# Weight-block sums of two later products: from VectorE to accumulating DMAs between DRAM buffers

## The chip, the cores and the metric

The kernel runs on one core of one Trainium2 chip. The metric is the device time of one execution in microseconds (us); lower is better. A difference of 0.3% is 4.7 us here.

## The reference

The kernel computes one hybrid encoder block on a sequence of 1024 frames with 16 learned tokens in front, model width 1024, all in float32. Cut to what matters here:

```
h  = concat(meta, x)                                  # 1040 x 1024
proj = rmsnorm(h) @ w_in                              # q, k, v, gates of 8 heads
for heads 0..3: mLSTM memory, in chunks               # causal conv on q and k, gated state
for heads 4..7: retention, in chunks                  # rotary q and k, decaying state
mixed = concat(normalised, gated outputs of 8 heads)  # 1024 x 2048
h  = h + mixed @ w_out                                # "w" product, w_out 2048 x 1024
u  = rmsnorm(h)
a  = silu(causal_dwconv(u @ w_up)) * (u @ w_gate)     # width 2816
h  = h + a @ w_down                                   # "d" product, w_down 2816 x 1024
out = rmsnorm(h)[16:]
```

## The kernel before

Every matrix product is made in three TensorE passes on operands that are split into a rounded high part and a low remainder (ScalarE copies the high part, VectorE subtracts it to get the low part). Tile schedules the program: each engine has one queue, worked in order, and waits on semaphores. All of the kernel's DMAs but one go out on SyncE's queue (SP); GpSimd's queue (POOL) has a few memsets at the start and two multiplications at the very end.

**The mixers** take the span from the start to about 700 us. Head after head, `o_group` (output gates) and `v_group` and `qk_group` of the next head are TensorE's main work, and the chunks of the scan (`scan_a`, `scan_b`, `post_steps`) are laid between them by `merge`. `need` and `issue` load a weight tile some units ahead; the raw tiles of all these weights share two buffers (tag `raw`), so that a load waits until the tile two loads back has been used up: `raw_v` of a head waits for the `raw_m` tile that `last_two` (L179) reads on VectorE. `tables` (L527, L528) loads the decay tables A1 and A2 of heads 0 to 3 from DRAM, 512 KB each with every row sent to all partitions, and VectorE adds the mask (L532).

**The two later products** are made by `class Seven`: a block product of 2 x 2 blocks with seven products in place of eight (Strassen and Winograd's form). The product "w" (w_out) follows the mixers from about 700 us, the product "d" (w_down) ends the kernel from about 1320 us. Four of the seven products need sums of weight blocks. In block form the weights of one step k are four tiles of 128 x 512: w11, w21, w12, w22. The steps named "65" and "73" each read a pair of sums from DRAM (`sums`, [128, 1024] for each product, step name and k); "w" has 8 of k, "d" has 11, and the steps "1", "2" and "4" (`QUARTER`) read blocks as they are. `rsplit` splits the activation side, `give` (L689) adds a finished PSUM bank to the residual.

**The sums** are made during the mixers: `wsum(g, k)` is called 19 times, up to three times with each head (after q pieces 0 and 2 and k piece 1 of heads 1 to 7). It loads two rows of blocks, 512 KB each (L189, L190), makes four VectorE operations on 128 x 512 (L192 to L195; the first is ordered behind the latest rescaling of q or k, `last["qk"]`), and stores four results of 256 KB each (L197).

Of the kernel before, what the change touches and what calls it, by code (L numbers as in the profile page):

```python
# [10 lines left out]
F32 = mybir.dt.float32  # L11
F32R = mybir.dt.float32r
AF = mybir.ActivationFunctionType
ALU = mybir.AluOpType
# [3 lines left out]
P = 128  # L18
# [12 lines left out]
HB = 4 * P  # L31
# [30 lines left out]
def body(ctx, tc, h_in, vecs, cst, mask_in, rot, w_v0, w_v, w_fm, w_out, w_up, w_gate, w_down, out):  # L62
    nc = tc.nc
# [9 lines left out]
    def after(later, first):  # L73

        tc.add_manual_dep(later.ins, first.ins.name, mybir.DependencyInfo(mybir.DependencyClass.NoSync, mybir.DependencyReason.DATA),
                          reason="order")

    last = {}
    V, G = nc.vector, nc.gpsimd
# [7 lines left out]
    accp = accseg.enter_context(tc.tile_pool(name="accp", bufs=1, side="right"))  # L87
# [96 lines left out]
    sums = {(g, st, k): dram.tile([P, 2 * HB], F32, name=f"ws{g}{st}_{k}") for g, n in (("w", 8), ("d", KD)) for st in ("65", "73") for k in range(n)}  # L184

    def wsum(g, k):
        src, n = (w_out, 8) if g == "w" else (w_down, KD)
        a, b = (accp.tile([P, 2 * HB], F32, tag=f"rr{i}", name=f"ws{g}{k}_{i}") for i in range(2))
        nc.sync.dma_start(a, src[k])  # L189
        nc.sync.dma_start(b, src[k + n])  # L190
        w11, w21, w12, w22 = a[:, :HB], a[:, HB:], b[:, :HB], b[:, HB:]
        after(nc.vector.tensor_tensor(w22, w21, w22, ALU.add), last["qk"])  # L192
        nc.vector.tensor_tensor(w21, w21, w11, ALU.subtract)
        nc.vector.tensor_tensor(w11, w22, w11, ALU.subtract)
        nc.vector.tensor_tensor(w12, w12, w11, ALU.subtract)  # L195
        for st, i, x in (("65", 0, w11), ("65", 1, w22), ("73", 0, w12), ("73", 1, w21)):
            nc.sync.dma_start(sums[g, st, k][:, i * HB:(i + 1) * HB], x)  # L197

    wsums = [(g, k) for g, n in (("w", 8), ("d", KD)) for k in range(n)]

# [34 lines left out]
    def fsplit(nm, srcs):  # L235
        return wsplit(*split_tiles(nm), srcs)

    def wsplit(hi, lo, srcs):
        o = 0
        for x in srcs:  # L240
            n = x.shape[1]
            nc.scalar.copy(hi[:, o:o + n], x)  # L242
            nc.vector.tensor_tensor(lo[:, o:o + n], x, hi[:, o:o + n].bitcast(F32), ALU.subtract)  # L243
            o += n
        return hi, lo
# [29 lines left out]
    def gained(kb, t0, t1, gcol, dve=False):  # L275
        g = vec[:, gcol + kb:gcol + kb + 1]
        if dve:
            nc.vector.tensor_scalar(uh[kb][:, t0:t1], resid[:, kb, t0:t1], g, None, ALU.mult)
        else:
            nc.scalar.activation(uh[kb][:, t0:t1], resid[:, kb, t0:t1], AF.Copy, scale=g)  # L280
        return nc.vector.scalar_tensor_tensor(ul[kb][:, t0:t1], resid[:, kb, t0:t1], g, uh[kb][:, t0:t1].bitcast(F32), ALU.mult, ALU.subtract)
# [33 lines left out]
    st = mix.enter_context(tc.tile_pool(name="st", bufs=1))  # L315
# [17 lines left out]
    A1 = st.tile([P, T], F32, name="A1")  # L333
    A2 = st.tile([P, T], F32, name="A2")
# [220 lines left out]
            m.append(nc.tensor.matmul(pt, al, xh_, start=False, stop=last and k == n - 1, skip_group_check=True))  # L555
        return m[0], m[-1]

    def rsplit(x, tiles, late=False):
        hi, lo = (t[:, :x.shape[1]] for t in tiles)
        m = nc.scalar.copy(hi, x), V.tensor_tensor(lo, x, hi.bitcast(F32), ALU.subtract)  # L560
        if late:
            behind(m)
        else:
            last["rsplit"] = m
        return hi, lo

    def behind(m):

        for x, y in zip(m, last["rsplit"]):
            after(x, y)  # L570

    def half_of(u, o):
        return tuple(y[:, o * HB:(o + 1) * HB] for y in u)

    class Seven:
# [54 lines left out]
        def prep(self, t):  # L630

            if t >= len(self.steps) or t in self.ops:
                return
            st, k = self.steps[t]
            nm = f"{self.nm}{st}_{k}"
            d = self.draws.get(t, {})
            act = self.act
            if st == "4" and self.order[-1] != "4":
                if t not in self.four:
                    self.pre4(t)  # L640
                r = rsplit(act["A1", k], self.rt(st, k, 0))
                self.ops[t] = [(self.four[t], r, "x")]
            elif st == self.order[-1]:
                if k % 2 == 0:
                    self.w = d.get("w")
                w = self.four.get(t) or wsplit(*self.wlast(k), [self.w[:, k % 2 * HB:(k % 2 + 1) * HB]])
                self.ops[t] = [(w, self.rhalf(k, 0), "xy"[st == "2"])]
            elif st in self.QUARTER:
                if k % 2 == 0:
                    self.w = fsplit(nm, [d["w"]])  # L650
                r = rsplit(act[{"1": "A1", "2": "A2", "4": "A1"}[st], k], self.rt(st, k, 0))
                self.ops[t] = [(half_of(self.w, k % 2), r, "xy"[st == "2"])]
            elif st == "65":
                a1, a2, b2 = (act[q, k] for q in ("A1", "A2", "B2"))
                r5 = rsplit(a1, self.rt(st, k, 1))
                V.tensor_tensor(a1, b2, a1, ALU.subtract)
                w = fsplit(nm, [d["l"]])
                r6 = rsplit(a1, self.rt(st, k, 0))
                V.tensor_tensor(a1, a2, a1, ALU.subtract)
                self.ops[t] = [(half_of(w, 0), r6, "x"), (half_of(w, 1), r5, "y")]  # L660
            else:
                w = fsplit(nm, [d["l"]])
                r7 = rsplit(act["B1", k], self.rt(st, k, 0))
                r3 = rsplit(act["B2", k], self.rt(st, k, 1))
                self.ops[t] = [(half_of(w, 1), r7, "x"), (half_of(w, 0), r3, "y")]
            self.read(t)

# [21 lines left out]
        def give(self, st):  # L689

            for b, j0, half in self.GIVE[st]:
                for j in range(4):
                    V.tensor_tensor(self.rs(j + j0, half), self.banks[b, j], self.rs(j + j0, half), ALU.add)

        def last_quarter(self, i, done):

# [271 lines left out]
    for i, (t0, t1) in enumerate(NP):  # L968
        for kb in range(KB):
            x = gained(kb, t0, t1, V_MIX, dve=kb < 4 if i == 0 else i > 1 and kb % 4 == 0)  # L970
# [19 lines left out]
    for h in range(8):  # L990
        A = lambda c, h=h: (lambda: scan_a(h, c))
        B = lambda c, h=h: ab(h, c)
        merge([lambda b=b, p=p: o_group(h, b, p) for b in range(2) for p in range(3)],
              [A(0)] + [B(c) for c in range(4 if h < 7 else NCH)])
        if h == 7:
            break
        side = post_steps(h, 0) + [B(4), B(5), B(6)] + post_steps(h, 1) + [B(7), B(8)] + post_steps(h, 2)
        merge([lambda c=c: v_group(h + 1, c)() for c in range(NCH)], side)
        tables(h + 1)
        for kind in "qk":  # L1000
            for p in range(3):
                qk_group(h + 1, kind, p)
                if (kind, p) in (("q", 0), ("q", 2), ("k", 1)) and wsums:
                    wsum(*wsums.pop(0))
# [141 lines left out]
    for t, (st, k) in enumerate(mixw.steps):  # L1146
# [4 lines left out]
        if st == "65" and k == 1:  # L1151
            x = fp.tile([P, 4 * XW], F32, name="wm", tag="xh2", bufs=1)
# [175 lines left out]
    def up_part(i):  # L1328
        chunks = UC
        def done(m, half, c):  # L1330
            if isinstance(c, list):
                t = ftile(f"c{i}_{m}{half}")
                for x, (j0, j1) in zip(c, chunks):
                    nc.scalar.copy(t[:, j0:j1], x)
                c = t
            conv(i, m, half, c)
        return seven("up", i, chunks, done)

    def gate_part(i):
        def done(m, half, c):  # L1340
            gate(i, m, half, c[0] if isinstance(c, list) else c[:, :HALF])
        return seven("ga", i, [(2, XW)], done)
# [50 lines left out]
    for i in range(1, NPAIR):  # L1393
        u, g = up_part(i), gate_part(i)
# [8 lines left out]
        if 2 < i:  # L1403
            kb = i - 3
# [90 lines left out]
    for p in (1, 2):  # L1495
# [5 lines left out]
        else:  # L1501
            for mb in (1, 4):
                x = resid[:, mb, OP[2][0]:OP[2][1]]
# [84 lines left out]
```

## Time and profile before

| | us |
|---|---|
| median of 3 runs | 1552.7 (1549.5 to 1554.35) |
| span of the profiled execution | 1551.5 |
| PE busy (TensorE matmul) | 1518.8 |
| DVE busy (VectorE) | 1124.2 |
| ACT busy (ScalarE) | 737.2 |
| POOL busy (GpSimd) | 2.4 |
| DMA queue of SP, share of 16 engines' span | 38.2% |

The profiled execution is given by its span, from the first to the last instruction; the runs' median lies 1.2 us above it. In the views, PE is TensorE's matmuls and PEld its weight loads, a trailing q means the sequencer of an engine, L12 is a line of the kernel, "x" counts instructions, and an arrow "<-" between two names of tiles is "out from in". In a row of waits the numbers are the idle us in total, how often, and the longest.

### The profile page before, as it was taken

The numbers are of one execution on the slowest core, as the hardware profiler recorded it, in microseconds if no ns is written. First come the engines' busy times: TensorE is split into PE (matmuls) and PEld (weight loads), VectorE is DVE, ScalarE is ACT, GpSimd is POOL, SyncE is SP. The second block draws the span as 40 slices with busy tenths as digits, with TensorE's granted clock in tenths as the row PEclk, the third lists the DMA queues.
The fourth block names the chain that finished last, engine by engine and source line by source line (L and its number), as shares of the span: only waits on it lengthen the run. The fifth ranks groups of instructions, "written<-read, shape, count | busy, mean of one in ns | idle before, by whom it ended". The sixth has DMA issues, their size and how long they took to land.

```text
span 1551.5 us, 25426 instructions
## 1 busy us (share of the span) xinstructions
PE 1518.8 (98%) x9763; PEld 1395.5 (90%) x9763; DVE 1124.2 (72%) x2388; ACT 737.2 (48%) x1493; POOL 2.4 (0%) x12
## 2 busy tenths in 40 slices
PE   8999999999999999999999999999999999999997
PEld 8989999999989999998788998999999999888887
DVE  8757768696767767678867778666666666778657
ACT  7574655455243343436454455444444444434443
POOL 0000000000000000000000000000000000000000
PEclk9999999999999999999999999999999999999999
DMA  6125435263533525226542326332222224923313
GB/s 219 36 70 163 152 110 188 79 218 97 181 122 126 167 85 189 94 91 245 177 139 100 101 78 195 96 102 89 82 80 78 82 82 137 385 96 116 95 42 109
DMA packets 92441, 197.41 MB, mean 127 GB/s; under 512 B 9048, under 2 KB 31264, under 8 KB 92320
## 3 DMA queue, kind: packets, MB, share of 16 engines
q1 hardware_dynamic: 92176, 195.73, 38.2%
q8 instruction: 76, 1.25, 0.3%
q14 instruction: 45, 0.37, 0.1%
q10 hardware_dynamic: 144, 0.07, 0.0%
HBM read 146.44 MB, written 49.32 MB: 126 GB/s over the span
## 4 chain that ended last, share of the span: by engine, by line
PE 87%; DMA 5%; DVE 4%; ACT 2%; issue 1%; SPq 0%; DVEq 0%; ACTq 0%
PE pv L373 4%; PE pv L374 4%; PE pv L375 3%; PE po L385 3%; PE po L384 3%; PE po L383 3%; PE pdx L553 3%; PE pdx L555 3%; PE pdx L554 3%; PE pup_x L554 2%; PE pup_x L555 2%; PE pga_x L553 2%; PE pga_x L555 2%; PE pga_x L554 2%; PE pup_x L553 2%; DMA A<-scr 2%
## 5 line engine op out<-in xcount | busy, mean ns | idle before, releaser
L373 PE MATMUL pv<-hi_v,uh 128*128 128x256 f32 (+1 forms) x512 | 147.1, 288 | 6.1 <-DVE vl L349 1.9
L374 PE MATMUL pv<-lo_v,uh 128*128 128x256 f32 (+1 forms) x512 | 146.6, 287 | 0.0
L375 PE MATMUL pv<-hi_v,ul 128*128 128x256 f32 (+1 forms) x512 | 146.0, 286 | 0.0
L383 PE MATMUL po<-uh,hi_o 128*128 128x386 f32 (+2 forms) x384 | 125.7, 327 | 0.0
L384 PE MATMUL po<-ul,hi_o 128*128 128x386 f32 (+2 forms) x384 | 123.9, 323 | 0.0
L385 PE MATMUL po<-uh,lo_o 128*128 128x386 f32 (+2 forms) x384 | 123.6, 322 | 0.0
L373 PEld LDWEIGHTS pv<-hi_v,uh 128*128 128x128 f32 x512 | 97.8, 191 | 10.1 <-issue 2.9
L374 PEld LDWEIGHTS pv<-lo_v,uh 128*128 128x128 f32 x512 | 97.7, 191 | 0.6 <-DVE lo_v L150 0.5
L375 PEld LDWEIGHTS pv<-hi_v,ul 128*128 128x128 f32 x512 | 97.7, 191 | 0.1
L242 ACT CAST hi_up<-raw_up 128x512 fp32r<-128x512 f32 (+1 forms) x52 | 36.5, 719 | 108.2 <-PE pga_z L554 61.0
L383 PEld LDWEIGHTS po<-uh,hi_o 128*128 128x128 f32 x384 | 72.9, 190 | 0.2
L384 PEld LDWEIGHTS po<-ul,hi_o 128*128 128x128 f32 x384 | 72.8, 190 | 0.2
L385 PEld LDWEIGHTS po<-uh,lo_o 128*128 128x128 f32 x384 | 72.7, 189 | 0.1
L243 DVE TENSOR_TENSOR lo_ga<-fraw_ga,hi_ga 128x512 fp32r<-128x512 f32 (+1 forms) x52 | 41.8, 807 | 36.9 <-ACT hi_ga L242 36.8
L553 PE MATMUL pup_x<-uh_g,hi_up 128*128 128x256 f32 (+1 forms) x240 | 67.2, 282 | 1.2 <-ACT uh_g L1021 1.2
L554 PE MATMUL pup_x<-ul_g,hi_up 128*128 128x256 f32 (+1 forms) x240 | 67.4, 283 | 0.1
L243 DVE TENSOR_TENSOR lo_up<-raw_up,hi_up 128x512 fp32r<-128x512 f32 (+1 forms) x52 | 41.2, 809 | 35.1 <-ACT hi_up L242 34.3
L383 PE MATMUL pq<-uh,hi_q 128*128 128x400 f32 (+2 forms) x192 | 63.2, 329 | 3.1 <-DVE vl L349 1.9
L555 PE MATMUL pup_x<-uh_g,lo_up 128*128 128x256 f32 (+1 forms) x240 | 66.2, 282 | 0.0
L383 PE MATMUL pk<-uh,hi_k 128*128 128x400 f32 (+2 forms) x192 | 62.3, 324 | 0.5 <-DVE rq L404 0.5
L243 DVE TENSOR_TENSOR lo_d<-rd,hi_d 128x1024 fp32r<-128x1024 f32 (+1 forms) x34 | 37.7, 1112 | 34.0 <-ACT hi_d L242 34.0
L384 PE MATMUL pq<-ul,hi_q 128*128 128x400 f32 (+2 forms) x192 | 62.1, 324 | 0.0
(747 smaller groups left out, 4981.4 us busy)
## 6 DMA issues: line engine op xcount, KB each, us to landing
wsd<-w_down_d SPq DMA_DIRECT2D x22, 512.0 KB, 4.1
wsd<-wsd SPq DMA_DIRECT2D x44, 256.0 KB, 2.5
raw_up<-w_up_d SPq DMA_DIRECT2D x22, 512.0 KB, 3.7
fraw_ga<-w_gate_d SPq DMA_DIRECT2D x22, 512.0 KB, 3.6
acts<-cv SPq DMA_DIRECT2D x44, 256.0 KB, 2.0
rd<-wsd SPq DMA_DIRECT2D x22, 512.0 KB, 3.3
wsw<-w_out_d SPq DMA_DIRECT2D x16, 512.0 KB, 4.3
raw_o<-w_fm_d SPq DMA_DIRECT2D x16, 512.0 KB, 3.5
```

What stands on the lines that cost most here:

```text
L242: nc.scalar.copy(hi[:, o:o + n], x)
L243: nc.vector.tensor_tensor(lo[:, o:o + n], x, hi[:, o:o + n].bitcast(F32), ALU.subtract)
L373: nc.tensor.matmul(pv[:L, :nv], a, hi[:, o:o + nv], start=kb == 0, stop=False)
L374: nc.tensor.matmul(pv[:L, :nv], a, lo[:, o:o + nv], start=False, stop=False)
L375: nc.tensor.matmul(pv[:L, :nv], b, hi[:, o:o + nv], start=False, stop=kb == KB - 1)
L383: nc.tensor.matmul(pt[:, :n], a, uh[kb][:, t0:t1], start=kb == 0, stop=False)
L384: nc.tensor.matmul(pt[:, :n], a, ul[kb][:, t0:t1], start=False, stop=False)
L385: nc.tensor.matmul(pt[:, :n], b, uh[kb][:, t0:t1], start=False, stop=kb == KB - 1)
L553: m.append(nc.tensor.matmul(pt, ah, xh_, start=first and k == 0, stop=False, skip_group_check=True))
L554: nc.tensor.matmul(pt, ah, xl_, start=False, stop=False, skip_group_check=True)
L555: m.append(nc.tensor.matmul(pt, al, xh_, start=False, stop=last and k == n - 1, skip_group_check=True))
```

## The change

`wsum` no longer brings the blocks into SBUF. It writes the sums in DRAM by DMA alone, in a form of the seven products in which all sums are additions. For each k there are seven DMAs from DRAM to DRAM:

- on SP, two plain ones of 512 KB, which put w21 into both halves of the "65" and of the "73" pair (the source is read twice, 2 KB rows);
- on POOL, five that add to what is in DRAM: w22 to both halves of "65", w11 to both halves of "73" (512 KB each), then w11 to the first half of "65", and w22 and w12 to the first half of "73" (256 KB each).

Each accumulating DMA waits for the one before it on the same bytes. The signs that the subtractions had go to the activation side: `rsplit` gets a form with `minus` (ScalarE multiplies by -1, VectorE uses a scalar_tensor_tensor) for step "1" and for the second operand of "73", and `give` subtracts two of the banks.

```diff
     def wsum(g, k):
         src, n = (w_out, 8) if g == "w" else (w_down, KD)
-        a, b = (accp.tile([P, 2 * HB], F32, tag=f"rr{i}", name=f"ws{g}{k}_{i}") for i in range(2))
-        nc.sync.dma_start(a, src[k])
-        nc.sync.dma_start(b, src[k + n])
-        w11, w21, w12, w22 = a[:, :HB], a[:, HB:], b[:, :HB], b[:, HB:]
-        after(nc.vector.tensor_tensor(w22, w21, w22, ALU.add), last["qk"])
-        nc.vector.tensor_tensor(w21, w21, w11, ALU.subtract)
-        nc.vector.tensor_tensor(w11, w22, w11, ALU.subtract)
-        nc.vector.tensor_tensor(w12, w12, w11, ALU.subtract)
-        for st, i, x in (("65", 0, w11), ("65", 1, w22), ("73", 0, w12), ("73", 1, w21)):
-            nc.sync.dma_start(sums[g, st, k][:, i * HB:(i + 1) * HB], x)
+        w11, w21, w12, w22 = (src[k + n * kb, :, mb * HB:(mb + 1) * HB].rearrange("p (i j) -> p i j", i=1) for kb in range(2) for mb in range(2))
+        x65, x73 = (sums[g, st, k].rearrange("p (i j) -> p i j", j=HB) for st in ("65", "73"))
+        both = lambda v: v.to_broadcast([P, 2, HB])
+        for x in (x65, x73):
+            nc.sync.dma_start(x, both(w21))
+        for x, v in ((x65, both(w22)), (x73, both(w11)), (x65[:, 0:1], w11), (x73[:, 0:1], w22), (x73[:, 0:1], w12)):
+            nc.gpsimd.dma_start(x, v, accum_op=ALU.add)
...
-    def rsplit(x, tiles, late=False):
+    def rsplit(x, tiles, late=False, minus=False):
         hi, lo = (t[:, :x.shape[1]] for t in tiles)
-        m = nc.scalar.copy(hi, x), V.tensor_tensor(lo, x, hi.bitcast(F32), ALU.subtract)
+        if minus:
+            m = nc.scalar.mul(hi, x, -1.0), V.scalar_tensor_tensor(lo, x, -1.0, hi.bitcast(F32), ALU.mult, ALU.subtract)
+        else:
+            m = nc.scalar.copy(hi, x), V.tensor_tensor(lo, x, hi.bitcast(F32), ALU.subtract)
...
-                    V.tensor_tensor(self.rs(j + j0, half), self.banks[b, j], self.rs(j + j0, half), ALU.add)
+                    x = self.rs(j + j0, half)
+                    V.tensor_tensor(x, x, self.banks[b, j], ALU.add if j0 or st == "2" else ALU.subtract)
```

More of the change, by code (lines that the diff above doesn't have):

```diff
@@ L650, in prep @@
                     self.w = fsplit(nm, [d["w"]])
-                r = rsplit(act[{"1": "A1", "2": "A2", "4": "A1"}[st], k], self.rt(st, k, 0))
+                r = rsplit(act[{"1": "A1", "2": "A2", "4": "A1"}[st], k], self.rt(st, k, 0), minus=st == "1")
                 self.ops[t] = [(half_of(self.w, k % 2), r, "xy"[st == "2"])]
@@ L663, in prep @@
                 r7 = rsplit(act["B1", k], self.rt(st, k, 0))
-                r3 = rsplit(act["B2", k], self.rt(st, k, 1))
+                r3 = rsplit(act["B2", k], self.rt(st, k, 1), minus=True)
                 self.ops[t] = [(half_of(w, 1), r7, "x"), (half_of(w, 0), r3, "y")]
```

## The prediction

> **What bounds the kernel now.** I read the page first, the span and the busy shares.
>
> ```profile
> span 1551.5 us, 25426 instructions
> PE 1518.8 (98%) x9763; PEld 1395.5 (90%) x9763; DVE 1124.2 (72%) x2388; ACT 737.2 (48%) x1493; POOL 2.4 (0%) x12
> ```
>
> TensorE is busy 98% of the span, so nothing that VectorE loses is a gain by itself: only idle time of PE can be won. The windows by stage say where that is (us, then busy us and count of each engine, granted clock, DMA share, GB/s).
>
> ```profile
> 0.00:128.00 128.00, 117.69 (x840) 111.33 (x841) 90.68 (x268) 84.27 (x185) 1.03 (x10) 0.99 0.32 106
> 128.00:697.00 569.00, 559.93 (x4035) 546.45 (x4034) 420.62 (x1084) 254.43 (x577) 0.00 (x0) 0.99 0.43 139
> 697.00:900.00 203.00, 200.85 (x1106) 172.03 (x1104) 156.71 (x293) 103.70 (x199) 0.00 (x0) 1.00 0.43 147
> 1320.00:1551.50 231.50, 223.48 (x1111) 187.38 (x1109) 161.88 (x257) 96.58 (x161) 1.41 (x2) 0.99 0.40 139
> ```
>
> All sums are made in the second stretch, the mixers of heads 1 to 7. There PE is idle for 569.00 - 559.93 = 9.1 us. PE's waits in that stretch are these, complete:
>
> ```profile
> PE tr L896 <- DVE mx L903: 2.7, 3, 1.5
> PE n L818 <- ACT num L852: 2.4, 1, 2.4
> PE pq L383 <- DVE vl L349: 1.9, 2, 1.2
> PE n L818 <- ACT S_0h L780: 1.3, 1, 1.3
> PE pk L383 <- DVE rq L404: 0.5, 1, 0.5
> PE n L820 <- DVE pt_1l L781: 0.2, 1, 0.2
> ```
>
> They sum to 9.0 us and fall into three kinds. (a) Rows 1 and 5, 3.2 us: PE waits for mx or rq, which stand behind the sums in VectorE's order. (b) Rows 2 and 6 in head 4 and row 4 in head 2, 2.6 and 1.3 us: PE waits for work behind a late `raw_v`. (c) Row 3, 1.9 us: PE waits for vl, which stands behind the mask add that waits for the table A. The timelines show the three places (start us, us, what, in brackets the idle time before it):
>
> ```profile
> 318.00 0.68 DVE L195 TENSOR_TENSOR wsw<-wsw,wsw 128x512 f32<-128x512 f32 x1
> 318.60 0.61 DVE L903 SCALAR_TENSOR_TENSOR mx<-tr,vec,sig 128x384 f32<-128x384 f32 x1
> 319.27 0.33 PE L896 MATMUL tr<-cs,num 128*128 128x128 f32 x1 [0.60 <-DVE mx L903]
> 424.26 0.69 DVE L192 TENSOR_TENSOR wsd<-wsd,wsd 128x512 f32<-128x512 f32 x1 [3.55 <-DMA wsd<-w_down_d]
> 258.17 0.42 SPq L146 DMA_DIRECT2D raw_v<-w_v_d  x1
> 430.68 0.33 SPq L190 DMA_DIRECT2D wsd<-w_down_d  x1
> 431.06 0.42 SPq L146 DMA_DIRECT2D raw_v<-w_v_d  x1
> 438.27 1.04 ACT L149 CAST hi_v<-raw_v 128x1024 fp32r<-128x1024 f32 x1 [6.66 <-DMA raw_v<-w_v_d]
> 219.33 1.23 DVE L532 TENSOR_TENSOR A<-A,mask 128x1024 f32<-128x1024 f32 x1 [4.83 <-DMA A<-scr]
> ```
>
> Seen here: mx starts the moment the fourth sum ends; a sum that waits 3.55 us for its load holds up all of VectorE; and `raw_v` goes out, in head 4, right behind the second load of 512 KB for a sum (L190) and takes 438.27 - 431.06 = 7.2 us.
>
> **The change part by part.** *VectorE.* The 76 operations go, and these rows (the mixers' window for the two tiles alone) give their time: 21.9 + 30.2 = 52 us of 420.62.
>
> ```profile
> 128.00:697.00 569.00, 21.91 (x32) 0.99 0.43 139
> 128.00:697.00 569.00, 30.15 (x44) 0.99 0.43 139
> ```
>
> On the path of it are only kinds (a) and (b). For (a) four sums of 0.6 us net stand ahead of an mx that PE missed by 0.6 to 1.5 us: 2.4 us is more than each of the three gaps, so I take all of it, **-3.2 us**; the bound on the other side is 0, if something else in VectorE's order ends as late. For (b), `raw_v` waits for the `raw_m` buffer, which VectorE frees (L179) after the sums. In head 2 (raw_v out at 258.17) four sums go ahead of it, 2.4 us; in head 4 four sums and the wait of 3.55 us, 5.9 us. So it goes out that much earlier.
>
> *DMA traffic.* Rows of the same stretch (KB each, median us from issue to landing):
>
> ```profile
> wsd<-w_down_d SPq DMA_DIRECT2D x22, 512.0 KB, 4.1
> wsd<-wsd SPq DMA_DIRECT2D x44, 256.0 KB, 2.5
> ...
> raw_v<-w_v_d SPq DMA_DIRECT2D x12, 512.0 KB, 4.9
> ...
> A<-scr SPq DMA_DIRECT2D x5, 512.0 KB, 7.2
> ```
>
> Each sum set moves 2 x 512 + 4 x 256 = 2048 KB now; then 2 x 512 plain and 2 x 512 + 3 x 256 = 1792 KB accumulating, 2816 KB. No row shows an accumulating DMA. At the least it costs as a copy; then 19 x 768 KB = 14.9 MB come on top, which at 139 / 0.43 = 323 GB/s is 46 us of all engines, share 0.43 to 0.51. At twice a copy, 19 x 2560 KB = 49.8 MB, 154 us, share 0.70. Neither fills the engines, but each load beside it shares them: `raw_v`, 4.9 us in the median and 7.2 us beside two loads, may land anywhere from as now to 7.2 us later (doubled). I take +2 us, near the lower end, since the plain copies stand exactly where the loads stood. Head 2: 1.3 - 2.4 + 2 leaves 0.9 of the gap; head 4: 5.9 - 2 is more than 2.6, all of it goes. Kind (b) gives **-3.0 us** (bounds: -3.9, and +6.1 if both land 7.2 us later, 1.3 - 2.4 + 7.2 and 2.6 - 5.9 + 7.2 against 3.9 now).
>
> *POOL.* Its queue has nothing else between the 10 memsets of the first stretch and the 2 multiplications of the last, so its waits delay only sums. One set takes, from the chain on the "73" bytes, 4.1 + 2.5 + 2.5 = 9.1 us at copy rate, 18.2 us at twice that, plus 4.1 us for the plain copy where that isn't early. The sums are due late:
>
> ```profile
> L602 SPq DMA_DIRECT2D raw_w<-wsw x4: 320/320/320, 719.5 to 732.4; - x4
> L602 SPq DMA_DIRECT2D rd<-wsd x22: 319/320/338, 1358.9 to 1471.2; - x22
> L197 SPq DMA_DIRECT2D wsw<-wsw x32: 319/320/327, 137.8 to 332.6; - x32
> ```
>
> From 137.8 the 8 sets of w have until 719.5, 73 us each: no wait there; without that cover TensorE would stand still for what is missing. On SP six issues a set become two, none of which waits; today its stores wait for L192 to L195. What they held up is `raw_v`, counted above. POOL's sequencer takes the five others.
>
> *The tables.* The next thing that can be late is A, since PE already waits behind it twice (kind (c)):
>
> ```profile
> 210.18 1.00 SPq L528 DMA_DIRECT2D A<-scr  x2
> 298.59 1.00 SPq L528 DMA_DIRECT2D A<-scr  x2
> 226.65 3.63 SPq L197 DMA_DIRECT2D wsw<-wsw  x4
> ```
>
> Three sets begin at 137.8 and three at 226.65, so the accumulations are over before A is loaded if a set takes under (210.2 - 137.8) / 3 = 24 us and (298.6 - 226.65) / 3 = 24 us. My bounds, 9 to 22 us, lie below it: **0**, with the other case as a rival. The Trainium skill, "Collectives: The Full Stack", section "The bandwidth ceiling: the fold count and why AG ≠ RS ≠ AR", says that an adding DMA runs at half the rate of a copying one because it reads two sources; by that rule the upper of my two rates holds, 22 us a set, and the margin is 2 us. No trace here shows it yet.
>
> *The signs.* 38 splits (8 + 11 in step "1", as many in "73") change form. Rows of the old forms and the nearest to the new ones (min/median/max ns):
>
> ```profile
> L560 DVE TENSOR_TENSOR rr<-wa,rr x32: 418/683/693, 706.3 to 854.0; 128x512 fp32r<-128x512 f32 x28, 128x256 fp32r<-128x256 f32 x4
> L1025 DVE SCALAR_TENSOR_TENSOR xl<-resid,vec,xh x16: 473/613/749, 862.7 to 904.7; 128x514 fp32r<-128x514 f32 x8, 128x256 fp32r<-128x256 f32 x4, 128x258 fp32r<-128x258 f32 x4
> L560 ACT CAST rr<-wa x32: 402/616/624, 705.2 to 853.0; 128x512 fp32r<-128x512 f32 x28, 128x256 fp32r<-128x256 f32 x4
> L1024 ACT ACTIVATE xh<-resid,vec x16: 494/609/727, 858.6 to 902.5; 128x514 fp32r<-128x514 f32 x8, 128x256 fp32r<-128x256 f32 x4, 128x258 fp32r<-128x258 f32 x4
> 705.89 0.50 PE L553 MATMUL pwx<-rr,hi_w 128*128 128x512 f32 x1 [0.17 <-ACT rr L560]
> ```
>
> VectorE: 749 - 683 = 66 ns each, 2.5 us in all; ScalarE: 727 - 616 = 111 ns, 4.2 us. They lie in stretches where DVE is busy 156.71 of 203 and 161.88 of 231.5 us, beside PE. Exposed are the first splits of each product, for which PE waits already (0.17): about 0.15 us twice, **+0.3 us** (0 to 6.7). The operations of `give` only swap operands: 0.
>
> Sum: -3.2 - 3.0 + 0 + 0.3 = -5.9 us. On the profiled span that is 1551.5 - 5.9 = 1545.6; the median stands 1.2 us above that span, so **1546.8 us**. A comparison can tell about 0.3%, 4.7 us, from no change: 1548.0 and 1557.4 are the limits.
>
> **The rivals.** *Half of it comes back.* `raw_v` lands 4 us later instead of 2: kind (b) then gives 3.9 - (1.3 - 2.4 + 4) - (2.6 - 5.9 + 4) = 0.3 us. Left is -3.2 - 0.3 + 0.3 = -3.2, **1549.5**. For it: `raw_v` already needs 7.2 us beside two loads; against it: the traffic is spread over more time.
>
> *The tables come late: slower.* A set takes more than 24 us, as when the DMA engines add at a third of the copy rate (27 us and more). A then shares the engines with accumulations at 210 and 299. VectorE already waits for A and PE behind it, so each us that A is late is a us of PE idle. At half as long again, 7.2 x 0.5 = 3.6 us twice, and `raw_v` 5 us later, (b) is 3.9 + 1.7 us against 3.9 now, and the sum -3.2 + 0.3 + 7.2 + 1.7 = +6.0, 1558.7; with both twice as long, -2.9 + 14.4 + 6.1 = +17.6, 1570.3. I put it at **1560**. It decides from 24 us a set. Against it: 22 us is the most that rows give. For it: no accumulating DMA is in the trace, and POOL must write the descriptors of five of them a set.
>
> *VectorE shares a port with POOL.* VectorE's two-elements-a-cycle operations, if they had to wait while POOL writes descriptors, would give back the first kind. In the q and k pieces of a head there are 6 of L407, 0.42 us each; at one issue of 0.33 us (SP's row) lost on each, 2.0 us come back to a stretch from which 12 x 0.6 = 7.2 us of sums went, 28% of the relief: -4.2 remain, **1548.5**. The Trainium skill, "SBUF — State Buffer", section "Who interferes with whom", states such an exclusive lock; no run here shows it, POOL being idle.
>
> *More is won*: kind (c) goes too, and all of (b), -9.0 + 0.3: **1544.0**, if less traffic meets the tables.
>
> **How the numbers follow.** Forecast 0.36, more won 0.07; half comes back 0.27, the port 0.05; tables late 0.25. Faster by over 0.3%: 0.43; within: 0.32; slower: 0.25, all of it taken as over 0.3%, though a mild case would be within. The forecast's own range is 1544.5 to 1548.0. Range: from 1543 to 1560, which leaves out the worse half of the slow case, 0.13, and 0.03 below.
>
> **What would show it.** Right: no DVE rows of L192 to L195; PE's waits for mx and rq gone; `raw_v` out near 256 and 425; the chain of one set on POOL under 24 us; PE idle in 128 to 697 us near 3 us. Wrong: VectorE's wait for A over 4.83 us, `raw_v` landing over 9 us, ScalarE's wait for hi_w at 707 or hi_d later than now, or accumulations still in flight at 210 and 299.

## The result, and the profile after

The changed kernel took 1593.8 us (median of 4 runs, 1592.1 to 1595.6), the kernel before 1551.1 us (4 runs beside them, 1548.2 to 1554.4): a ratio of 1.0272, 95% interval 1.0252 to 1.0291. It is 2.7% slower, where 0.4% faster was forecast. These lines of the page answer to those of before.

```profile
span 1590.3 us, 25319 instructions
PE 1530.3 (96%) x9763; PEld 1404.1 (88%) x9763; DVE 1086.0 (68%) x2312; ACT 727.6 (46%) x1485; POOL 89.8 (6%) x107
PEclk9879999999999999999999999999999999999999
...
q1 hardware_dynamic: 86096, 175.80, 33.5%
q0 software_dynamic: 18544, 34.87, 14.1%
```

VectorE lost its 76 operations (2388 to 2312; 1124.2 to 1086.0 us). PE issues the same 9763 matmuls, yet is busy 11.5 us longer, and the granted clock dips in slices 2 and 3. So the loss lies near the start, before the stage in which the sums were made. The windows give the place (us, busy time and count of each engine, granted clock, DMA share, GB/s). A DMA share of 1 means that all 16 engines are busy; the view's figure can lie a little over 1.

```profile
40.00:60.00 20.00, 19.62 (x126) 19.19 (x125) 15.10 (x48) 8.24 (x17) 2.08 (x2) 1.00 1.04 306
60.00:80.00 20.00, 8.81 (x54) 7.45 (x52) 9.53 (x40) 6.46 (x11) 1.03 (x1) 0.72 1.03 272
80.00:100.00 20.00, 6.51 (x23) 6.51 (x24) 1.23 (x1) 2.33 (x2) 2.09 (x2) 0.52 1.04 306
```

From 60 to 100 us PE is busy 15 of 40 us, while all 16 DMA engines are full. The timeline of SP's queue says with what (start us, us, instruction, count):

```profile
9.34 3.73 SPq L192 DMA_DIRECT2D wsw<-w_out_d  x2
...
15.58 25.00 SPq L192 DMA_DIRECT2D wsw<-w_out_d  x13
40.62 36.98 SPq L192 DMA_DIRECT2D wsd<-w_down_d  x16
77.76 1.06 SPq L146 DMA_DIRECT2D raw_o<-w_fm_d  x1
79.44 11.18 SPq L192 DMA_DIRECT2D wsd<-w_down_d  x6
...
95.85 13.82 SPq L146 DMA_DIRECT2D raw_v<-w_v_d  x2
```

All 38 plain copies of the 19 sets go out between 9 and 91 us. Head 0's load of raw_o stands behind 32 of them, the last 16 in a row, and goes out at 77.76; in the kernel before it goes out at 29.9 us:

```profile
29.91 7.12 SPq L146 DMA_DIRECT2D raw_o<-w_fm_d  x2
```

A copy goes out only every 36.98 / 16 = 2.3 us. Issuing one takes 1.2 us in the median of the 22 of w_down (0.61 us in e1 below, where the engines are not full). The rest is waiting: each copy also waits for the landing of the DMA eight places before it in SP's queue (the issues at 44.55, 46.58 and 47.77 follow landings at 44.53, 46.48 and 47.75). SP's waits from 15 to 92 us:

```profile
SPq L192 <- DMA wsw<-w_out_d: 8.1, 9, 2.0
SPq L192 <- DMA wsd<-w_down_d: 7.1, 7, 1.8
```

So full engines slow the queue, and the load behind the copies goes out late. raw_o then takes 14.2 us to land instead of 3.5. PE's waits, first those up to 130 us, then those of 128 to 697 us:

```profile
PE po L380 <- ACT hi_o L149: 17.8, 1, 17.8
PE pf L490 <- ACT A L488: 3.6, 1, 3.6
...
PE pe L473 <- DVE A L470: 1.7, 1, 1.7
...
PE pt L508 <- DVE A L505: 1.2, 1, 1.2
```

```profile
PE pq L380 <- DVE vl L346: 4.6, 2, 4.3
PE u L819 <- ACT kwh L802: 3.8, 2, 2.4
```

One wait for the late raw_o costs 17.8 us. Without its output gates, which run from 63.5 us in the kernel before, head 0 has nothing to put between the steps that make the tables, so the three waits for A, 6.5 us, lie bare. The granted clock is 0.50 from 70 to 99.2 us, so it outlasts the long wait, which ends at 93.5: up to 99.2 us the output-gate matmuls follow each other every 0.32 us, from there on every 0.18. By the start of the first q matmul of head 1 the changed kernel is 33.5 us behind (165.5 against 132.0 us). The windows up to there, before and after:

```profile
0.00:132.00 132.00, 121.69 (x861) 115.33 (x862) 93.41 (x273) 86.87 (x192) 1.03 (x10) 0.97 0.32 105
0.00:165.50 165.50, 129.91 (x860) 121.19 (x861) 92.76 (x273) 77.76 (x181) 17.94 (x26) 0.89 0.89 246
```

PE is idle for 35.6 us instead of 10.3, and about the same matmuls take 8.2 us longer: 25.3 + 8.2 = 33.5. Heads 1 to 4 take 355.9 instead of 350.3 us, +5.6; from there to the end the two are equal (1068.9 and 1069.2 us). That is the whole difference of 38.8 us between the spans.

### The profile page after: what moved, and what is told of

It is laid out like the page before. It is cut to its first block, busy times and chain, and to the rows that moved or that the text cites. A ratio compares the mean times of both kernels' runs of the same rounds, so it can differ in the third digit from the quotient of the medians.

```text
span 1590.3 us, 25319 instructions
## 1 busy us (share of the span) xinstructions
PE 1530.3 (96%) x9763; PEld 1404.1 (88%) x9763; DVE 1086.0 (68%) x2312; ACT 727.6 (46%) x1485; POOL 89.8 (6%) x107
## 3 DMA queue, kind: packets, MB, share of 16 engines
q1 hardware_dynamic: 86096, 175.80, 33.5%
q0 software_dynamic: 18544, 34.87, 14.1%
## 4 chain that ended last, share of the span: by engine, by line
PE 83%; DMA 10%; DVE 3%; ACT 2%; issue 1%; SPq 1%; DVEq 0%; ACTq 0%
PE pv L370 3%; PE po L382 3%; PE po L380 3%; PE po L381 3%; PE pv L371 3%; PE pv L372 3%; PE pdx L550 3%; PE pdx L552 3%; PE pdx L551 3%; PE pup_x L551 2%; PE pup_x L552 2%; PE pga_x L550 2%; PE pga_x L552 2%; PE pga_x L551 2%; PE pup_x L550 2%; DMA wsd<-w_down_d 2%
## 5 line engine op out<-in xcount | busy, mean ns | idle before, releaser
L380 PE MATMUL po<-uh,hi_o 128*128 128x386 f32 (+2 forms) x384 | 126.0, 328 | 17.8 <-ACT hi_o L149 17.8
L424 DVE TENSOR_TENSOR sig<-po,Rb 128x386 f32<-128x386 f32 (+2 forms) x48 | 24.5, 511 | 61.1 <-PE po L382 61.0
L425 ACT ACTIVATE sig<-sig 128x386 f32<-128x386 f32 (+2 forms) x48 | 23.5, 490 | 88.2 <-DVE sig L424 88.1
```

Of the source, the lines that this page charges most:

```text
L380: nc.tensor.matmul(pt[:, :n], a, uh[kb][:, t0:t1], start=kb == 0, stop=False)
L424: nc.vector.tensor_tensor(s, pt[:, :n], Rb[:, t0:t1], ALU.mult)
```

## The experiments

In the kernel before, three things kept a set in its place: its loads wrote to the two SBUF buffers `rr0` and `rr1`, which had to be free; its first sum was ordered by `after(..., last["qk"])` behind the latest q or k piece; and its stores waited for the sums. The change takes all three away. A copy from DRAM to DRAM has no buffer and no predecessor, so nothing orders it behind the place in the program where it is written. The theories: (1) the place of the copies in SP's queue ahead of head 0's loads makes the loss; (2) the traffic, of the adds above all, costs time whenever it comes; and, added once e1 had come out as (1) says and e2 as (2) says, (3) copies and adds together, unheld, fill all 16 engines, and head 0's loads land late. The first four kernels ran on one chip, the next four on another. Where heads are timed below, it is in one profiled execution of each kernel, and such times scatter: the mixers of e4 are those of the kernel before, and its heads 1 to 4 take 346.8 us against 350.3.

**e1, the plain copies held in their places.**

```diff
-            nc.sync.dma_start(x, both(w21))
+            after(nc.sync.dma_start(x, both(w21)), last["qk"])
```

> The changed kernel, with one edit: each of the 38 plain copies on SP is ordered behind the latest rescaling of q or k, as the first sum of each set was before; the accumulating DMAs on POOL are as changed. Theory 1 (place in the queue): the 42 us come from the plain copies, which nothing held back, so that all 38 stood at the head of SP's queue between 9 and 91 us, ahead of the loads of the first head. Then this kernel lies at the prediction's level, 1545 to 1555 us, PE has no idle time over 5 us, and head 0 reaches its output gates at about 64 us as before. Theory 2 (traffic): the adding DMAs move twice the bytes and slow every load of the mixers. Then most of the loss stays, 1575 to 1595 us.

1549.0 us (1547.4 to 1551.6, 6 runs) against 1553.4 (21 runs): ratio 0.9969, interval 0.9958 to 0.9981. One ordering turns 2.7% slower into 0.3% faster than before; this version beats both kernels. `after` sets no semaphore, it only fixes an order in the schedule: the first two copies now go out at 134.89 us, right behind a load of raw_m at 134.51. Its window, all PE waits from 128 to 697 us of 0.5 us or more, and its DMA queues there:

```profile
128.00:697.00 569.00, 565.81 (x4105) 554.39 (x4104) 388.45 (x1030) 257.91 (x591) 88.40 (x95) 1.00 0.75 169
```

```profile
PE pv L370 <- DVE vl L346: 1.6, 1, 1.6
PE u L819 <- ACT kwh L811: 1.4, 1, 1.4
PE pwx L550 <- ACT rr L558: 1.1, 1, 1.1
PE pq L380 <- DVE vl L346: 0.5, 1, 0.5
```

```profile
q0 software_dynamic: 18544, 34.87, 40.5%
q1 hardware_dynamic: 31054, 60.80, 33.8%
...
raw_v<-w_v_d SPq DMA_DIRECT2D x12, 512.0 KB, 7.1
```

The same 34.87 MB of adds and a DMA share of 0.75 now lie beside PE with 3.2 us of idle time, where before had 9.1. So traffic as such is not what costs 40 us: theory 2 falls. Heads 1 to 4 take 340.8 us, 9.5 less than before. More than half of that is given back from head 5's first q matmul to the end (1074.6 against 1069.2 us). Of these 5.4 us 4.1 are longer busy times of the same matmuls, at a granted clock of 0.99 instead of 1.00. The product of w takes 162.5 us, 3.2 more than before; but it takes 162.4 us in e3 too, which makes no sums, so this part is not shown to be the adds' doing.

**e2, the copies unheld, without the adds.** The five accumulating DMAs are deleted.

> The changed kernel without its 95 accumulating DMAs (the sums hold w21 alone); the plain copies float to the head of SP's queue as in the changed kernel. Theory 1: the copies alone make the loss of the first 130 us, some 30 us; 1575 to 1590 us. Theory 2: without the adding DMAs the loss is gone; 1550 to 1560 us.

1554.9 us (8 runs), ratio 1.0009 (0.9993 to 1.0025). SP's queue looks as in the changed kernel, only shorter:

```profile
36.56 27.37 SPq L192 DMA_DIRECT2D wsd<-w_down_d  x16
64.81 0.40 SPq L146 DMA_DIRECT2D raw_o<-w_fm_d  x1
```

Head 0's raw_o still stands behind 32 copies, but the last 16 go out every 1.7 us instead of every 2.3. It goes out 13 us earlier than in the changed kernel, and ScalarE splits it at 77.2 instead of 92.4 us. PE waits 3.8 us for it, not 17.8, beside the same three waits for A. Against e3 the copies cost 12 us, not the 40 of theory 1; the time lies in the range of theory 2. e1 spoke for theory 1 and against theory 2, this kernel the other way round. Both fit only if it takes copies at the head and adds together: theory 3.

**e3, no sums at all.** `wsum` returns at once, and steps "65" and "73" load the plain blocks.

> The changed kernel with no sums made at all: no copies, no accumulating DMAs, no VectorE sums; the steps 65 and 73 load the first row of weight blocks in place of the sums. It bounds what the change can win. By the prediction's waits, 7.1 us of PE's idle time belong to the sums, so 1543 to 1546 us; if the waits of the tables go too, 1541 us. If VectorE's sums cost nothing but these waits are replaced by others, 1549 to 1553 us.

1542.9 us (4 runs), ratio 0.9928 (0.9913 to 0.9942): 10.5 us less than before, the sign forms included. The row of this kernel's windows:

```profile
128.00:697.00 569.00, 568.07 (x4120) 556.55 (x4118) 391.58 (x1031) 262.28 (x596) 0.00 (x0) 1.00 0.24 75
```

PE's idle time in the mixers falls from 9.1 to 0.9 us. This is what the relief of VectorE is worth when no DMA pays for it. Heads 1 to 4 take 339.0 us, only 1.8 less than in e1; most of the 6 us between the two kernels lies outside these heads, beside which 12 of the 19 sets are made.

**e4, the signs alone.** The kernel before with `rsplit`'s minus form and the new `give`.

> The kernel before with the sign forms of the change alone: rsplit with minus for step 1 and for the second operand of 73, and subtraction in two of the gives; the sums stay on VectorE in their old form, so the output is that of other weights. The prediction has +0.3 us (0 to 6.7). If the forms take VectorE or ScalarE time that PE waits for, up to +6.7 us.

1554.0 us (10 runs), ratio 1.0009 (0.9995 to 1.0023): nothing that can be told from zero, and at most 3.6 us.

**e5, copies unheld, each add waits for its q or k piece.**

```diff
-            nc.gpsimd.dma_start(x, v, accum_op=ALU.add)
+            wait(nc.gpsimd.dma_start(x, v, accum_op=ALU.add), last["qk"])
```

> The changed kernel, where the 38 plain copies still float to the head of SP's queue, but each accumulating DMA waits by semaphore for the latest rescaling of q or k, so that the adding goes on from about 140 us, set by set with the heads. The copies at the head alone cost little against the kernel before (1.0009 of its time), and the copies in their places with the adds cost nothing. Theory 3 (both at once): the loss comes from adds and copies that fill the engines together in the first 130 us, and from loads that stand behind those copies in SP's queue. Then head 0 reaches its output gates at about 78 us, as with copies alone, heads 1 to 4 take about 341 us as with ordered copies, and the time is 1556 to 1563 us. Theory 2 (the adds' traffic, whenever it comes): 1580 us or more.

1566.6 us (1564.9 to 1568.6, 4 runs) against 1552.9 (19 runs), ratio 1.0088 (1.006 to 1.0116); just over the 1556 to 1563 of theory 3, far from theory 2. Head 1 begins at 144.3 us, as in e2 (143.2), where the changed kernel has 165.5. So of the 33 us up to head 1, 12 are the copies', and 21 come only when the adds run beside them. Heads 1 to 4 take 347.7 us, 6.9 more than in e1 with the same adds in the same heads; that part was not expected. The longest wait of PE there, 3.2 us for num at 300.2 us, follows a late raw_q: it goes out at 287.43, and ScalarE, 6.8 us idle for it, splits it at 295.61. Why it is late is not shown, and two executions of held kernels differ by more (340.8 us in e1, 350.3 in e8's profile, whose run of 1553.1 us is the slowest of its ten).

**e6, the copies taken from SP and issued by POOL,** behind its last memset, unordered; the adds follow in the same queue.

> The changed kernel with the 38 plain copies issued by POOL, behind its last memset, and unordered otherwise; the adds are on POOL as before. The traffic comes as early as in the changed kernel, but nothing of it stands in SP's queue. If the place in SP's queue makes the loss (theory 1), head 0 reaches its output gates at 64 to 68 us and the time is 1548 to 1556 us. If the filled engines make it (theory 3), the loads of head 0 land late all the same: output gates at 75 us or later, 1565 us or more.

1588.2 us (1576.2 to 1590.1, 4 runs), ratio 1.0201 (1.015 to 1.0252). With no copy in SP's queue almost all of the loss stays, so a place in that queue is not needed for it. SP's rows and the longest PE wait in heads 1 to 4:

```profile
4.60 6.87 SPq L947 DMA_DIRECT2D cs<-cst_d  x1
...
12.00 10.05 SPq L945 DMA_DIRECT2D resid<-h_in_d  x2
22.18 9.58 SPq L146 DMA_DIRECT2D raw_q<-w_fm_d  x1
```

```profile
PE pq L380 <- DVE vl L346: 9.9, 4, 6.3
```

Some of SP's own issues now take 5 to 10 us with nothing of the change ahead of them (0.65, 3.32 for two, and 0.35 us in the kernel before), while the engines, filled from another queue, show a share of 0.97 up to 40 us. The path is not quite that of the changed kernel: here the copies start at 1.5 us instead of 9.3 and hit the first loads of all, those of the input and of raw_q. Head 0's first q matmul comes at 55.0 us instead of 37.3, its output gates at 84.8 (75 or later was expected), and PE waits 0.6 us for raw_o, not 17.8. So e6 shows that full engines alone can make such a loss; how the 17.8 us of the changed kernel divide between a late issue and a slow landing it does not show.

**e7, four sets a head** (heads 1 to 5) in the ordered form, so that adds are still running when A is loaded: the slow rival of the prediction.

> The kernel with ordered copies, but with four sets of sums in each of heads 1 to 5 (after q pieces 0 and 2 and k pieces 0 and 1) in place of three in heads 1 to 7. A set took 24 us there, three of them end just before the tables A are loaded at about 211 and 292 us; four take 97 us of a head's 85, so adds are in flight when A is loaded. Prediction's slow rival: A then lands 3 to 6 us later, twice, and PE waits as long: 1554 to 1561 us. If sharing costs the tables nothing: 1547 to 1551 us.

1560.8 us (1553.0 to 1569.8, 10 runs), ratio 1.0054 (1.0029 to 1.0078), 12 us over e1. VectorE's wait for A at head 2 in e1 and in e7, and e7's three longest PE waits:

```profile
219.69 1.23 DVE L529 TENSOR_TENSOR A<-A,mask 128x1024 f32<-128x1024 f32 x1 [4.46 <-DMA A<-scr]
```

```profile
223.43 1.23 DVE L529 TENSOR_TENSOR A<-A,mask 128x1024 f32<-128x1024 f32 x1 [11.38 <-DMA A<-scr]
```

```profile
PE tr L897 <- DVE mx L904: 5.9, 2, 4.9
PE u L819 <- ACT kwh L802: 4.9, 1, 4.9
PE u L819 <- ACT kwh L811: 3.3, 1, 3.3
```

The wait for A at head 2 grows by 6.9 us and comes out as PE's 4.9 us for mx; at head 3 it does not grow (4.62 us against 4.37 in e1). The other two waits, 8.2 us, follow splits of raw_v in ScalarE's order, before which ScalarE sat idle for raw_v for 1.9 and 7.1 us; raw_v lands up to 17.0 us after issue, in e1 up to 9.4. The rival had both terms, A twice and raw_v less, so its mechanism is real, but that its sum comes out so well is partly luck. The changed kernel was not slow through it.

**e8, fewer bytes:** 1280 KB of adds a set instead of 1792.

> The kernel with ordered copies, and 1280 KB of adding a set in place of 1792 KB: w21 goes to both halves of 65 and to the second half of 73 alone; the first half of 73 is copied from the finished first half of 65 (POOL, plain) and w12 added. Same sums. The traffic of copies and adds costs 1549.0 - 1542.9 = 6 us against no sums at all; if that goes with the bytes added, 1546 to 1548 us and a set in about 20 us. If what is left comes from something else, 1548 to 1550 us.

1548.9 us (10 runs), ratio 0.9977 (0.9963 to 0.9991): as e1, though the two ran on different chips. A gain of 2 us or more from the fewer bytes does not show, which speaks against them as what keeps e1 from e3's time.

**e9, one burst in heads 1 and 2.** All copies are held only behind the first q group of head 1. On a third chip, with e10.

```diff
+        last.setdefault("head1", last["qk"])
-            after(nc.sync.dma_start(x, both(w21)), last["qk"])
+            after(nc.sync.dma_start(x, both(w21)), last["head1"])
```

> All 38 plain copies are held back only behind the first q group of head 1 (about 133 us); from there on nothing paces them, nor the adds behind them. Copies and adds together take some 19.9 MB at the 316 GB/s and 34.87 MB at the 151 GB/s of the ordered kernel, 63 and 231 us, so all engines are filled from about 133 us to 430 us or later. Theory 3 in its narrow form (the loss is that of head 0, whose loads of raw_o, raw_v and the tables A come while the engines are full): head 0 ends as in the ordered kernel (q of head 1 near 132 us), heads 1 to 4 lose what the changed kernel lost there beside the ordered one, 15 us, or less: 1549 to 1564 us. A wider theory (whatever stage the unpaced traffic falls on, its loads come late by as much as head 0's did): 30 us or more lost in heads 1 to 4, a granted clock under 0.9 in some of them, 1575 us or more. Theory 1 (only the place in SP's queue at the head of the program): as the ordered kernel, 1547 to 1552 us.

1603.0 us (1594.1 to 1605.5, 6 runs), ratio 1.0332 (1.0313 to 1.035): slower still than the changed kernel. Head 0 ends in time (q of head 1 at 131.5 us); head 1 takes 135.9 us instead of 85.4. SP's queue, VectorE's and PE's waits and the window show why:

```profile
165.46 43.54 SPq L193 DMA_DIRECT2D wsd<-w_down_d  x19
209.09 2.57 SPq L917 DMA_DIRECT2D mxd<-mx  x1
```

```profile
225.73 0.62 DVE L905 SCALAR_TENSOR_TENSOR mx<-tr,vec,sig 128x386 f32<-128x386 f32 x1 [30.16 <-DMA mxd<-mx]
```

```profile
PE tr L898 <- DVE mx L905: 31.2, 3, 28.2
```

```profile
200.00:300.00 100.00, 65.52 (x436) 61.31 (x437) 43.01 (x115) 30.78 (x66) 16.72 (x17) 0.78 0.83 183
```

This time it is the store of mx that waits behind 19 copies, one every 2.3 us. VectorE waits 30 us for its buffer, PE 28.2, and the clock falls: of the 50.5 us that head 1 loses against e1, 9.4 are longer busy times of PE. Theory 3 in its narrow form, that head 0 alone is hurt, falls; what holds is the wider form: copies and adds that nothing paces fill the engines, and whatever load or store of the stage comes then is late, wherever the burst falls.

**e10, two sets in each of heads 1 to 4, then 4, 4 and 3** in heads 5 to 7.

> The ordered kernel with two sets in each of heads 1 to 4 and four, four and three in heads 5 to 7, where no table A is read from DRAM any more. The ordered kernel stands 6 us over the kernel without any sums; its share of DMA time in heads 1 to 4 is 0.75 of the stage. If those 6 us are traffic beside the loads of heads 1 to 4: 1544 to 1548 us, PE's idle time in heads 1 to 4 under the 2.1 us of the ordered kernel. If four sets in a head crowd the loads whatever tables there are (the kernel with four sets in heads 1 to 5 was 12 us slower than the ordered one): 1552 us or more, lost after 473 us.

1559.2 us (1551.8 to 1567.3, 12 runs) against 1552.2 (17 runs), ratio 1.0047 (1.0027 to 1.0067). Heads 1 to 4 take 339.5 us, as without sums (339.0), and head 5 with four sets 83.4; but head 7's sets run into the product of w, which takes 173.7 us instead of the 162.5 of e1 and whose own loads fill the engines (share 0.97 to 1.03 from 705 to 720 us in the kernel before):

```profile
PE pwy L550 <- ACT hi_w L239: 3.6, 1, 3.6
PE pwx L550 <- DVE C L861: 2.7, 1, 2.7
```

**e11, three sets in heads 1 to 3, two in head 4, four in heads 5 and 6, none in head 7.**

> The ordered kernel with its 19 sets moved among the heads: three in each of heads 1 to 3, two in head 4, four in each of heads 5 and 6, none in head 7. From the traces so far: head 4 with two sets took 83.7 us against 85.6 with three (the tables from rot come there); head 5 took 83.4 with four sets, as with none; three sets in head 7 pushed into the product of w and cost some 9 us there. If the place of a set beside the loads of its own head is what costs: heads 1 to 4 within 1 us of the kernel without sums, nothing lost after it, 1544 to 1548 us. If four sets in a row cost in heads 5 and 6 after all: 1549 us or more, lost between 470 and 640 us.

1549.6 us (1546.1 to 1557.3, 12 runs, on a fourth chip) against 1552.1 (17 runs), ratio 0.999 (0.9975 to 1.0005): not better than e1. Neither expectation fits: heads 5 and 6 with four sets take 83.3 and 83.4 us, so nothing is lost there, but heads 1 to 4 take 344.2. Head 3, with the same sets at the same places as in e1, took 88.6 us here and 84.5 there. Differences of this size between e1, e8 and e11 belong to the execution, and I do not rank the three.

## Why the prediction was wrong

**The step that failed** is one sentence under *DMA traffic*: "the plain copies stand exactly where the loads stood", and with it, under *POOL*, "On SP six issues a set become two, none of which waits". The second half of that is the fault itself. What waits is also held. The loads stood where they stood because of their buffers and because the sums that freed these were ordered; the copies kept neither, went out from 9 us on, and drew the adds after them. The prediction nowhere asks what takes the place of `after(nc.vector.tensor_tensor(...))`, which goes with the VectorE work and was the anchor of the set's DMAs. e1 mends that line alone and moves the time from 1593.8 to 1549.0 us. A row of the kernel before gave the sign (min/median/max ns, first and last start in us):

```profile
L189 SPq DMA_DIRECT2D wsw<-w_out_d x8: 332/350/2970, 9.0 to 320.2; - x8
```

The first set's loads, whose buffers are free from the start, already went out at 9.0 us there, 128 us ahead of their sums.

**What the step costs.** e2 and e5 put 12 us on the copies at the head. The adds beside them bring head 1 from 143 or 144 us to 165.5 in the changed kernel. e6 shows that the copies need not stand in SP's queue for a loss of this size, e9 that it need not be head 0. In the changed kernel and in e9 the late load or store did stand behind copies on SP, in a queue that full engines had slowed.

**The bound on DMA traffic** was of the right kind and put in the wrong place. "Neither fills the engines" averaged the traffic over 569 us. Spread so (e1) the share is 0.75, near the upper bound of 0.70; unspread all engines are full from 20 to 100 us (1.03 to 1.05).

**The rate of the adds.** In e1 the adds take 0.405 of 569 us of all engines for 34.87 MB, 151 GB/s; the plain queue, with its loads, stores and copies, takes 0.338 for 60.80 MB, 316 GB/s. An add takes 2.09 times the plain traffic's time for each byte, about the upper of the two bounds. With that the trace agrees with the Trainium skill, "Collectives: The Full Stack", section "The bandwidth ceiling: the fold count and why AG ≠ RS ≠ AR", which has the adding step of a ring collective at half the rate of the copying one because the add reads two sources. The Trainium skill confirms this for rings of three or more ranks; for an adding DMA between two DRAM buffers e1 shows it.

**A set's time against 24 us.** In e1's timelines of POOL (first and last add of head 1's sets) and SP (the tables of heads 2 and 3):

```profile
141.37 1.20 POOL L194 DMA_DIRECT2D wsw<-w_out_d  x1 [139.81 <-DMA wsw<-w_out_d]
...
202.93 0.82 POOL L194 DMA_DIRECT2D wsw<-w_out_d  x1 [4.91 <-DMA wsw<-w_out_d]
```

```profile
210.90 1.00 SPq L525 DMA_DIRECT2D A<-scr  x2
292.01 5.03 SPq L525 DMA_DIRECT2D A<-scr  x2
```

The last add of three sets begins at 202.93, A goes out at 210.90, and the median landing of such an add is 5.8 us: a margin of 2 us. From the first copy at 134.89 the three sets take some 74 us, 24.6 each, so a set is longer than the upper bound of 22 and close to the limit, which by the same sum is (210.90 - 134.89) / 3 = 25.3 us here. For head 3's table there is no margin: the last add of head 2's sets begins at 289.4, and A goes out at 292.01 with that add in flight, one of the signs that the prediction named for being wrong. VectorE's waits for A are all the same 4.46 and 4.37 us (4.83 and 5.17 before), so **0** for the tables was right in the held kernel, though not for the reason given; e7 shows what lies beyond the limit.

**Terms (a) and (b), -3.2 and -3.0 us.** Right in kind, and visible only with the sets held. In e1 PE waits for neither mx nor rq, and for nothing behind raw_v in head 2. raw_v lands 7.1 us after issue in the median, 2.2 later than before, where the prediction took +2. In head 4 one takes 9.4 us, and the 1.4 us of kwh, which follows its split in ScalarE's order, remain of (b); the prediction had left 0.9, in head 2. So of PE's idle time in heads 1 to 4 all of (a) went, 3.2 us, 2.5 of (b) and 1.4 of (c), which the forecast left alone. e3 puts the whole relief at 10.5 us, a little above the 8.7 of the rival *more is won*. In e1 the heads win 9.5 us in the profiled execution, 7.0 of idle time and 2.5 of shorter matmuls, and 4.3 are left at the end of the comparison, against the forecast's 5.9. That these two lie so close is partly luck, since the 5.4 us lost after head 4 stand in no term.

**The signs, +0.3 us,** and `give`: e4 agrees with it but cannot tell it from zero; its interval reaches from -0.8 to +3.6 us, so the upper bound of 6.7 is out.

**The port between VectorE and POOL.** In e1 POOL is busy 88 us in the mixers, and the operations that such a lock would hold up (L404 there, L407 before) meet it only twice in 18 times. e10 has a clear case:

```profile
149.02 1.95 POOL L194 DMA_DIRECT2D wsw<-w_out_d  x2 [7.17 <-issue]
149.34 0.56 DVE L404 TENSOR_SCALAR cvk<-rk,vec 128x400 f32<-128x400 f32 x1
```

Over all traces 270 of these operations have no DMA instruction of POOL beside them; they take at most 435, 424 and 360 ns (400, 384 and 256 columns). Of 35 that begin while POOL is at one, 13 take longer than that, by at most 0.15 us; of 7 that POOL joins later none does. So there is a delay, but it is under half of the 0.33 us that the rival took, and not each time: in e1 one operation of 446 ns is all. The Trainium skill, "SBUF — State Buffer", section "Who interferes with whom", has whoever issues first hold the shared ports for its whole instruction. The order agrees with the traces, the length does not: POOL's instruction takes about 1 us and the longest delay is 0.15 us.

**POOL** spends more on an add than SP's 0.33 us, which the prediction took (e1, min/median/max ns):

```profile
L194 POOL DMA_DIRECT2D wsw<-w_out_d x30: 812/1055/1377, 141.4 to 289.4; - x30
```

Nothing else stands in its queue there, so this costs no more than part of the set's 24 us.

**The chances.** The slow side had 0.25, all of it for tables that come late. That mechanism did not decide, and its 1560 us was 34 us short. A rival "the DMAs run elsewhere than they are written" was missing.

## What to carry to other kernels

When an edit removes a wait, a buffer or an ordering from a DMA, ask what still holds it in its place, and if the answer is nothing, add an order of its own: here one `after` was worth 45 us. A transfer that has no due time was cheap here only while it was spread (DMA share 0.75 over the mixers, 3.2 us of idle PE) and dear in a burst (33.5 us by head 1, 50.5 us in e9's head 1); what counts is the share of the DMA engines in the stretch where it actually runs, and whose loads and stores stand behind it there. Judge a change with two effects by kernels that have one each: without the sums 10.5 us were to be had, with them held 4.3 came.

## What the hardware showed that was not expected

- With all engines full, SP's queue itself becomes slow: a copy goes out every 2.3 us in the changed kernel. Issuing one takes 1.2 us in the median and up to 4.9, against 0.61 in e1, and each copy waits until the DMA eight places before it has landed. In e6, where no copy stood on SP, the issue of raw_q took 9.6 us instead of 0.35.
- A late load costs nothing until its slack is used up, and then its full lateness. ScalarE splits raw_o at 37.3 us in the kernel before, 26 us ahead of the first output gate; at 77.2 in e2, where PE waits 3.8 us for it; and at 92.4, 15.2 us later, in the changed kernel, where PE waits 17.8.
- A long stall of PE is paid again in the clock. In the changed kernel it is granted at 0.50 from 70 us, while PE waits, until 99.2, 5.7 us after the long wait; in e9 it reads 0.51 from 226 to 237 us, right after the 28.2 us wait, and 1.00 from there to 245.
- VectorE's operations of L404 and a DMA instruction of POOL do meet: where POOL came first, 13 of 35 took longer than any without it, by up to 0.15 us.
